# A two-layer diffusion backbone on one core: late small loads, turned rows modulated from PSUM, root norms behind attention

## The chip, the core and the metric

The kernel runs on one core of one Trainium2 chip, in one launch. The metric is the device time of that launch in microseconds (us). A core has five engines that work beside each other, each through its own queue in order: TensorE (PE; its weight loads are shown apart as PEld), VectorE (DVE), ScalarE (ACT), GpSimd (POOL) and SyncE (SP), which here issues nearly all DMAs. Matrix products land in PSUM; operands lie in SBUF. Differences under about 0.2% of the time are not counted as a change.

## The reference

512 latent tokens and 256 context tokens of width 1024 pass two layers. Each layer is a mixer and a squared-ReLU MLP, both between RMS norms, with a shift, a scale and a gate made from the conditioning vector. Layer 0 mixes by pooling, layer 1 by attention; after layer 1 only the latent tokens are needed.

```python
def rms_norm(x, g):
    xf = x.astype(jnp.float32)
    y = xf * lax.rsqrt(jnp.mean(xf * xf, axis=-1, keepdims=True) + EPS)
    return (y * g.astype(jnp.float32)).astype(x.dtype)
...
def modulate(h, shift, scale):
    return h * (1.0 + scale) + shift
...
    for i in range(DEPTH):
        last = i == DEPTH - 1
        j = i // N_MIXERS
        sh1, sc1, gt1, sh2, sc2, gt2 = ada_mods(c, w_ada[i], b_ada[i])
        csh1, csc1, cgt1, csh2, csc2, cgt2 = ada_mods(c_ctx, w_ada[i], b_ada[i])
        h_lat = modulate(rms_norm(x, g_mix_pre[i]), sh1, sc1)
        h_ctx = modulate(rms_norm(ctx, g_mix_pre[i]), csh1, csc1)
        if i % N_MIXERS == 0:
            y_lat = pool_mixer(h_lat, w_pool[j], pool_scale[j])
            y_ctx = None if last else pool_mixer(h_ctx, w_pool[j], pool_scale[j])
        else:
            y_lat, y_ctx = attention_mixer(h_lat, h_ctx, w_qkv[j], g_q[j], g_k[j], w_o[j], not last)
        x = x + gt1 * rms_norm(y_lat, g_mix_post[i])
        m_lat = sq_relu_mlp(modulate(rms_norm(x, g_mlp_pre[i]), sh2, sc2), w_mlp_in[i], w_mlp_out[i])
        x = x + gt2 * rms_norm(m_lat, g_mlp_post[i])
...
    return x
```

`ada_mods` is SiLU of the conditioning vector times `w_ada` (1024 x 6144 for each layer). `pool_mixer` is, for each of four groups of 256 channels, a windowed mean less the token itself (windows of 2, 4, 8 and 16 tokens), a 256 x 256 product and a scale by channel. Attention has 8 query heads and 2 key heads of 128, with RMS norms and rotary positions on queries and keys.

## The kernel before

Tokens lie in six tiles of 128 rows (`t` = 0 to 3 latent, 4 and 5 context), channels in eight blocks of 128 (`k`). Float32 operands of the large products are split in a high part (rounded) and a low part (the rest); a product is then three matmuls: high by high, high by low, low by high. In tile names `ra` and `rb` hold such halves, `acc` and `work` float32 results, `raw` freshly loaded weights, `units` split weights.

The program has these stages, in us of the profiled execution:

- *Front* (0 to about 102). The conditioning maps come as 1 MB loads of `w_ada`, called units (scale, shift and gate: SC1, SH1, GT1 for the mixer, SC2, SH2 for the MLP). `ada_mm` multiplies them into `psada`, `ada_turn` transposes that on VectorE, `ada_sel` and `ada_add` make columns `mods`, and `avec` (gain times one plus scale). Means by band matrices land in `psm`, the mixer's products in `pspool`. `pool_m` copies a row tile of `pspool` to `acc`, `pool_q` takes its root mean square on ScalarE, `pool_b` multiplies it by the gate and `pool_r` adds it to the stream. `turn_c` scales a row tile by its own norm, `turn_pair` transposes two row tiles on PE into `psx`, `turn_ev` copies that to `acc`, `modulated` applies scale and shift, `placed` splits it into `hH` and `hL` (the `ra<-acc` rows). The first inner product of the MLP follows in two chunks: chunk 0 is the first four row tiles (`psin`, 512 wide), chunk 1 the last two (256 wide).
- *First MLP* (102 to 600), a Strassen-like scheme whose products read `units`.
- *Queries, keys, values and attention* (600 to 776). `q_a` projects a chunk of queries into `psq`, `q_e` and `q_b` norm and rotate it; `q_head` transposes a head (`pq`), `s_scores` makes scores (`pss`) and their exponential, `s_norm` divides by the sum, `s_turn` transposes (`pspt`), `s_values` multiplies by the values (`po`).
- *Output projection, norm, and the first inner product of the second MLP* (776 to 838), *second MLP* (838 to 1135), *tail* (to 1164): the last row tile's norm, residual and output DMAs.

What stands where in the front and in attention's output is a table of planned times: `st.at(time, function, ...)` collects calls, and `Steps.run` issues them in the order of these times. `pin` and the flag `fixed` hold the resulting order on an engine; elsewhere a scheduler decides. DMAs go through SP's queue in order with eight semaphores in rotation. Raw weights of the front come from a ring of four tiles (`rawe`), two of SH2's loads from another of three (`rawp`).

The row norms after attention and at the end are the mean square (ScalarE) and a power of -0.5 on GpSimd:

```python
    def rstd(ss, parts):
        r = sm_tile("rs")
        gp.tensor_tensor(out=r[:, 0:1], in0=ss[:, parts + 3:parts + 4], in1=nhalf[:, 0:1], op=ALU.pow)
        return r
```

Of the kernel before, what the change touches and what calls it, by code (L numbers as in the profile page):

```python
# [17 lines left out]
P = 128  # L18
# [35 lines left out]
def backbone(ctx: ExitStack, tc, x, c, ctx_in, c_ctx, w_ada, b_ada, g_mix_pre, g_mix_post,  # L54
# [152 lines left out]
    def mean_square(src, ss, n):  # L207
        z = sc.activation(junk[:, 0:src.shape[-1]], src, AF.Square, scale=float(D) ** -0.5, accum_out=ss[:, n:n + 1])
        sc.activation(ss[:, n + 4:n + 5], ss[:, n:n + 1], AF.Identity, bias=ss[:, n + 3:n + 4] if n else eps)
        return z  # L210
# [8 lines left out]
    def row_root(key, src):  # L219
        roots[key] = ss = sm_tile("ss")  # L220
        sc.activation(junk, src, AF.Square, scale=float(D) ** -0.5, accum_out=ss[:, 0:1])
        sc.activation(ss[:, 1:2], ss[:, 0:1], AF.Sqrt, bias=eps)
# [36 lines left out]
    sy.dma_start(pr1[0:96, :], row(b_ada))  # L259
    sy.dma_start(pr1[96:112, :], row(g_mix_pre))  # L260
    sy.dma_start(pr1[112:128, :], row(g_mlp_pre))
# [3 lines left out]
    te.transpose(pp[:, 0:128], pr1, ident)  # L265
# [3 lines left out]
    ve.tensor_copy(cols, pp[:, 0:128])  # L269
# [8 lines left out]

    def ada_mm(i, m, c0, width, u):
        nk = 2048 // width  # L280
        raw = raw_load(w_ada[i, u * nk * P:(u + 1) * nk * P, m * D + c0:m * D + c0 + width]
                       .rearrange("(k p) n -> p k n", p=P), width,
                       rawp if (m, c0, u) in ((SH2, 0, 1), (SH2, 512, 0)) else None).rearrange("p (k n) -> p k n", n=width)
# [129 lines left out]

    def modulated_pair(t, i, s, hi, lo, works, wide, fine, on_act):
# [20 lines left out]
        for q in range(4):  # L435
# [13 lines left out]
            elif q % 2:  # L449
# [3 lines left out]
                ve.tensor_tensor(out=place(lo, ks), in0=split2(h), in1=place(hi, ks), op=ALU.subtract)  # L453

    def last_pair(t, i, s, hi, lo, on_act):
        works, sh = [accv[:, t + u, :] for u in range(2)], (SH1, SH2)[s] * KT
        pss = [psB.tile([P, 2, 256], F32, tag="b", name="psx") for _ in range(KT // 2)]
        for u in range(2):
            for k in range(KT):
                te.transpose(pss[k // 2][:, k % 2, u * P:(u + 1) * P], works[u][:, k * P:(k + 1) * P], ident)  # L460
        for k in range(KT):
            src, h = pss[k // 2][:, k % 2, :], works[k // 4][:, 256 * (k % 4):256 * (k % 4) + 256]
            sa, b = avec[i][s][:, k, 0:1], mods[i][:, sh + k, 0:1]
            z = slice(t * P, (t + 2) * P)
            if on_act[k]:
                sc.activation(h, src, AF.Identity, scale=sa, bias=b)
            else:
                ve.tensor_scalar(out=h, in0=src, scalar1=sa, scalar2=b, op0=ALU.mult, op1=ALU.add)
            sc.copy(hi[:, k, z], h)
            ve.tensor_tensor(out=lo[:, k, z], in0=h, in1=hi[:, k, z], op=ALU.subtract)  # L470
# [10 lines left out]
    def mean_mm(k, q, narrow=False):  # L481
# [8 lines left out]
        for i in range(n):  # L490
            v = 0 if i == 0 else (1 if i == n - 1 else 2)
            lo = max(i * P - HALO, 0)
            hi = min((i + 1) * P + HALO, n * P)
# [65 lines left out]
    def pool_mul(g):  # L559
        w4 = pw[0][:, 512 * g:512 * g + 512].rearrange("p (k n) -> p k n", n=256)  # L560
        ve.tensor_tensor(out=w4, in0=w4, in1=pw[1][:, 256 * g:256 * g + 256].unsqueeze(1).broadcast_to([P, 2, 256]),
                         op=ALU.mult)

    def pool_hi(g):
        z = slice(512 * g, 512 * g + 512)
        sc.copy(wpH[:, z], pw[0][:, z])
# [18 lines left out]
    def pool_q(t):  # L585
        row_root((0, t), accv[:, t, :])

    def pool_b(t, n0=0, n1=D):
        gated(t, accv[:, t, :], accv[:, t, n0:n1], n0, n1)
# [7 lines left out]
    def norm_r(t, half=False):  # L597
        y = yg.pop(t, accv[:, t, :])
        for h in range(2 if half else 1):
            residual(t, y, *((512 * h, 512 * h + 512) if half else (0, D)))  # L600

    def norm_s(t, half=False):
        if not half:
# [3 lines left out]
        for h in range(2):  # L607
            mean_square(xrow(t)[:, 512 * h:512 * h + 512], ss, h)
        rs[t] = rstd(ss, 2)

    def norm_c(t, act, pool, half=False):
        r = rs[t][:, 0:1]
# [17 lines left out]
    accp = acc.rearrange("p (q k n) -> p q k n", q=NT // 2, n=256)  # L630
# [3 lines left out]
    def turn_pair(q):  # L634
        src = accv[:, 2 * q:2 * q + 2, :]
        if q < 2:
            both = [psA.tile([P, 4, 256], F32, tag="a", name="psx") for _ in range(2)]
            pss = [both[kk // 2][:, 2 * (kk % 2):2 * (kk % 2) + 2, :] for kk in range(4)]
        else:
            pss = [psB.tile([P, 2, 256], F32, tag="b", name="psx") for _ in range(4)]  # L640
        for kk, ps in enumerate(pss):
            for k in range(2):
                for u in range(2):
                    pin(te.transpose(ps[:, k, u * P:(u + 1) * P], src[:, u, (2 * kk + k) * P:(2 * kk + k + 1) * P], ident),
                        q < 2)
        faced[q] = pss

    def turn_ev(q, on_act, kks=range(4)):
        for kk in kks:
            ps = faced[q][kk]  # L650
            pin((sc.copy if on_act[kk] else ve.tensor_copy)(accp[:, q, 2 * kk:2 * kk + 2, :], ps), q < 2)

    def modulated(k, ci, on):
        qs = (slice(0, 2), slice(2, 3))[ci]
        h = accp[:, qs, k, :]
        sa, b = avec[0][1][:, k, ci:ci + 1], mods[0][:, SH2 * KT + k, ci:ci + 1]
        if on is sc:
            z = sc.activation(h, h, AF.Identity, scale=sa, bias=b)
        else:
            z = on.tensor_scalar(out=h, in0=h, scalar1=sa, scalar2=b, op0=ALU.mult, op1=ALU.add)  # L660
        pin(z, ci == 0)

    def placed(k, ci, low):
        qs = (slice(0, 2), slice(2, 3))[ci]
        h = accp[:, qs, k, :]
# [23 lines left out]
    class Inner:  # L689
        def __init__(self, g, w, aH, aL, hid, chunks_of, ntok):  # L690
# [3 lines left out]
            self.ps, self.r = {}, {}  # L694

        def part(self, c, f, ks=range(KT), on=False):
# [5 lines left out]
            for k in ks:  # L702
                for n, (w, a) in enumerate(((wH, aH), (wH, aL), (wL, aH))):
# [944 lines left out]
```

## Time and profile before

| quantity | value |
|---|---|
| time, median of 3 runs (lowest to highest) | 1165.27 us (1164.26 to 1166.16) |
| the profiled execution, its own time | 1165.85 us |
| its span in the profile | 1164.0 us |
| DVE / ACT / POOL busy, share of the span | 80% / 56% / 7% |
| moved by DMA | 152.08 MB |
| granted TensorE clock | 1.00 in every stage |

The page of the profile gives busy time by engine, then the span in 40 slices, the chain of work that ended last, and the costliest groups. A row of a timeline is: start, duration, engine, line, operation, out<-in, partitions x elements and type, count, and in brackets how long the engine was idle just before and which tile of which engine released it. Nearly all lines read L68, a helper through which every instruction goes, so rows are told apart by their tiles. Here are the 40 slices of PE, DVE and DMA:

```profile
PE   6989999999999999999999999999999999999997
...
DVE  4787587889989899898768689977787779778875
...
DMA  9994132334434434444442300045344224314303
```

### The profile page before, as it was taken

Reading aid. Unit: us, or ns where it says so; the run is one execution under the profiler, and the core shown is the slowest. Engines: PE = TensorE matmul, PEld = TensorE weight load, DVE = VectorE, ACT = ScalarE, POOL = GpSimd, SP = SyncE. Lnnn points to the kernel's source line nnn. Section 1 sums busy time; section 2 is a strip of 40 time slices with the busy share of each in tenths; the row PEclk is TensorE's granted clock in tenths of the full one; section 3 lists DMA queues with packets and bytes.
Section 4 is the critical chain, followed back from the end, with each engine's and each line's share of the span. In section 5 each row is a group of like instructions: output and inputs, shape, how many; then the busy total and the mean of one; then the engine's idle time right before and its main releaser. Section 6 shows DMA issues by size and latency. Waiting matters only on the chain. (4 is left out here: it accounts for less than half of the span.)

```text
span 1164.0 us, 15687 instructions
## 1 busy us (share of the span) xinstructions
PE 1137.8 (98%) x6026; PEld 981.5 (84%) x6026; DVE 936.0 (80%) x1540; ACT 649.4 (56%) x1152; POOL 80.7 (7%) x93
## 2 busy tenths in 40 slices
PE   6989999999999999999999999999999999999997
PEld 4659899989889988988888889988888888888886
DVE  4787587889989899898768689977787779778875
ACT  5586655545335434555795468862775436435524
POOL 1052000000000000000232210102000000000000
PEclk9999999999999999999999999999999999999999
DMA  9994132334434434444442300045344224314303
GB/s 337 399 334 162 49 104 84 125 114 143 160 127 145 145 113 145 140 135 146 183 152 79 120 1 1 14 139 170 131 140 150 70 75 145 109 37 146 109 31 114
DMA packets 95161, 152.08 MB, mean 131 GB/s; under 512 B 2880, under 2 KB 67952, under 8 KB 95088
## 3 DMA queue, kind: packets, MB, share of 16 engines
q1 hardware_dynamic: 94992, 151.07, 37.7%
q8 instruction: 47, 0.77, 0.3%
q14 instruction: 26, 0.21, 0.1%
q10 hardware_dynamic: 96, 0.02, 0.0%
HBM read 141.65 MB, written 9.44 MB: 130 GB/s over the span
## 5 line engine op out<-in xcount | busy, mean ns | idle before, releaser
L68 PE MATMUL pso<-units,rb 128*128 128x512 f32 x1152 | 277.2, 392 | 0.0
L68 PEld LDWEIGHTS pso<-units,rb 128*128 128x128 f32 x1152 | 214.9, 188 | 41.6
L68 DVE TENSOR_TENSOR acc<-acc,pso 128x512 f32<-128x512 f32 x192 | 128.9, 684 | 61.5 <-PE pso L68 61.4
L68 DVE SCALAR_TENSOR_TENSOR rows<-raw,cond,rows 128x256 f32<-128x256 f32 x280 | 122.3, 486 | 0.7
L68 PE MATMUL psin<-ra 128*128 128x512 f32 (+1 forms) x424 | 112.2, 369 | 0.0
L68 PE MATMUL psin<-ra,rb 128*128 128x512 f32 (+1 forms) x384 | 103.5, 362 | 3.6 <-DVE ra L68 1.8
L68 ACT CAST units<-raw 128x1024 fp32r<-128x1024 f32 (+2 forms) x71 | 70.7, 1018 | 39.9 <-PE pso L68 21.7
L68 DVE TENSOR_TENSOR units<-raw,units 128x1024 fp32r<-128x1024 f32 (+2 forms) x69 | 82.7, 1208 | 12.5 <-ACT units L68 12.4
L68 PE MATMUL psin<-rb,ra 128*128 128x384 f32 (+1 forms) x324 | 90.6, 356 | 0.0
L68 PEld LDWEIGHTS psin<-ra 128*128 128x128 f32 x424 | 77.8, 188 | 11.3 <-DVE work L68 0.3
L68 ACT ACTIVATE work<-psin 128x512 f32<-128x512 f32 (+3 forms) x66 | 36.2, 550 | 85.9 <-PE psin L68 78.7
L68 PE MATMUL psin<-ra,units 128*128 128x384 f32 x432 | 82.7, 336 | 0.4 <-ACT psin L68 0.4
L68 PE MATMUL pso<-units,pairs 128*128 128x512 f32 x336 | 82.3, 389 | 0.0
L68 PEld LDWEIGHTS psin<-ra,rb 128*128 128x128 f32 x384 | 66.9, 189 | 17.1 <-DVE ra L68 3.3
L68 POOL TENSOR_TENSOR rs<-ss,nhalf 128x1 f32<-128x1 f32 x30 | 21.2, 708 | 855.1 <-ACT ss L68 852.2
L68 PEld LDWEIGHTS psin<-ra,units 128*128 128x128 f32 x432 | 76.3, 188 | 3.1 <-ACT psin L68 0.5
L68 PEld LDWEIGHTS pso<-units,pairs 128*128 128x128 f32 x336 | 63.1, 188 | 13.1
L68 PE MATMUL psin<-sums,units 128*128 128x384 f32 x336 | 63.8, 336 | 0.0
L68 PEld LDWEIGHTS psin<-rb,ra 128*128 128x128 f32 x324 | 58.6, 188 | 5.6
L68 ACT COPY acc<-pso 128x512 f32<-128x512 f32 x68 | 38.0, 589 | 41.5 <-PE pso L68 41.4
L68 PEld LDWEIGHTS psin<-sums,units 128*128 128x128 f32 x336 | 59.0, 188 | 1.4
L68 ACT CAST rb<-raw 128x2048 fp32r<-128x2048 f32 (+2 forms) x20 | 27.0, 1349 | 58.0 <-PE pso L68 55.7
(223 smaller groups left out, 2151.6 us busy)
## 6 DMA issues: line engine op xcount, KB each, us to landing
raw<-in_w_ada SPq DMA_DIRECT2D x48, 1024.0 KB, 5.4
raw<-in_w_mlp_in SPq DMA_DIRECT2D x32, 1024.0 KB, 5.3
raw<-in_w_mlp_out SPq DMA_DIRECT2D x32, 1024.0 KB, 5.9
raw<-in_w_qkv SPq DMA_DIRECT2D x6, 1024.0 KB, 5.1
spill<-xl SPq DMA_DIRECT2D x8, 512.0 KB, 5.6
xl<-spill SPq DMA_DIRECT2D x8, 512.0 KB, 7.5
raw<-in_w_o SPq DMA_DIRECT2D x4, 1024.0 KB, 4.9
xl<-in_x SPq DMA_DIRECT2D x4, 512.0 KB, 6.9
```

Source lines behind the costliest of these rows:

```text
L68: z = made(*args, **kw)
```

## The change

1. *Loads.* `b_ada`, `g_mix_pre` and `g_mlp_pre` are loaded behind the two units of SC1's first half, and transposed (`small_turn`) when they are needed. Both loads of SH2's first half use `rawp`.
2. *Mixer.* The band products take only as many columns as their window reaches (`halo = 1 << g` in place of a fixed one). `pool_mul` and two of the four `pool_hi` go to GpSimd. Row tiles 3, 4 and 5 of the mixer are not copied out of PSUM: the root mean square and the gating read `pspool`.
3. *Turned rows.* `turn_ev` is gone. `modulated` reads `psx` in PSUM, one 128 x 256 piece for each `k` and pair of row tiles, 12 on ScalarE and 12 on VectorE (before: 512 wide pieces on three engines for chunk 0, eight 256 wide pieces on GpSimd for chunk 1). `first_part` issues, for each `k`, the matmuls that don't read the low half ahead of those that do. The table of times is rewritten around it.
4. *Attention.* The last query chunk is copied from PSUM by `q_rest`; its squares stand behind four of the exponentials, and its norm and rotation go to GpSimd. Behind the last exponential stands one square root on a single column, which loads ScalarE's table for roots. One of the four tiles of probabilities (`pbuf`) moves to another part of `acc`.
5. *Norms behind attention.* The norms of the output stage and of the end are a square root on ScalarE and a reciprocal on VectorE. Two low halves of the earlier pair are held back behind the residual of the last row tile (`late`), nine matmuls of chunk 0 are kept back until the last transposes are out (`hold`), and modulates alternate between the engines.
6. *Tail.* The last row tile leaves in three DMAs (512, 256, 256 columns) in place of two.

```diff
+    def settle(t):
+        if t in pending:
+            rs[t] = sm_tile("rs")
+            ve.reciprocal(rs[t][:, 0:1], pending.pop(t))
...
-        sc.activation(ss[:, n + 4:n + 5], ss[:, n:n + 1], AF.Identity, bias=ss[:, n + 3:n + 4] if n else eps)
+        sc.activation(ss[:, n + 4:n + 5], ss[:, n:n + 1], AF.Sqrt if root else AF.Identity, bias=ss[:, n + 3:n + 4] if n else eps)
...
+                if (i, s, q) == (1, 1, 3):
+                    late.extend((place(lo, z), h[:, z.start - 4:z.stop - 4], place(hi, z)) for z in (slice(4, 6), slice(6, 8)))
...
-        ve.tensor_tensor(out=w4, in0=w4, in1=pw[1][:, 256 * g:256 * g + 256].unsqueeze(1).broadcast_to([P, 2, 256]),
+        gp.tensor_tensor(out=w4, in0=w4, in1=pw[1][:, 256 * g:256 * g + 256].unsqueeze(1).broadcast_to([P, 2, 256]),
...
     def pool_b(t, n0=0, n1=D):
-        gated(t, accv[:, t, :], accv[:, t, n0:n1], n0, n1)
+        if t not in mix:
+            gated(t, accv[:, t, :], accv[:, t, n0:n1], n0, n1)
+        else:
+            halves = lambda z: z.rearrange("p (q n) -> p q n", q=2)
+            ve.tensor_tensor(out=halves(accv[:, t, :]), in0=mix.pop(t), in1=halves(gate[:, slot[t], :]), op=ALU.mult)
...
-    def modulated(k, ci, on):
-        qs = (slice(0, 2), slice(2, 3))[ci]
-        h = accp[:, qs, k, :]
+    def modulated(q, k, on):
+        h, ps, ci = accp[:, k // 2, k % 2, q, :], faced[q, k // 2][:, k % 2, :], q // 2
         sa, b = avec[0][1][:, k, ci:ci + 1], mods[0][:, SH2 * KT + k, ci:ci + 1]
         if on is sc:
-            z = sc.activation(h, h, AF.Identity, scale=sa, bias=b)
+            sc.activation(h, ps, AF.Identity, scale=sa, bias=b)
...
+    def first_part(c, k):
+        first[0].final = 1
+        for terms in ((0, 2), (1,)):
+            for f in range(2):
+                first[0].part(c, f, (k,), False, terms)
...
-    ada_units(SH2, 512, 512, (72.9, 73.9), 76.5, 77.9, 78.6)
+    ada_units(SH2, 512, 512, (70, 73.9), 74.8, 75.75, 76)
...
+    def q_rest(ch, t):
+        d = q32[:, t, 512 * ch:512 * ch + 512]
+        ve.tensor_copy(d, pj[ch, t])
+        pj[ch, t] = d
...
-        head_norm(ps, r, 4, 0, t, q32[:, t, 512 * ch:512 * ch + 512])
+        head_norm(ps, r, 4, 0, t, q32[:, t, 512 * ch:512 * ch + 512], gp if exps and t == NL - 1 else ve)
...
+        at(33.6, lambda: sc.activation(sm_tile("sm")[:, 7:8], smx[len(steps) - 1][:, 1:2], AF.Sqrt))
...
-        for n0, n1 in ((0, 512), (512, D)):
+        for n0, n1 in ((0, 512), (512, D)) if t < NL - 1 else ((0, 512), (512, 768), (768, D)):
```

On VectorE, at the end of the front, where the scale and shift columns are made (`psada` transposed, then `mods` and `avec`) and the first turned rows are modulated, before and then now:

```order
L68 STREAM_TRANSPOSE work<-psada 128x512
L68 TENSOR_TENSOR acc<-acc,gate 128x1024
L68 STREAM_TRANSPOSE work<-psada 128x512
L68 RECIPROCAL rs<-ss 128x1
L68 SCALAR_TENSOR_TENSOR xr<-acc,rs,xr 128x1024
L68 TENSOR_TENSOR rb<-raw,rb 128x512 x2
L68 TENSOR_TENSOR mods_96<-psada,cols 128x16
L68 SCALAR_TENSOR_TENSOR avec_99<-mods_96,cols 128x16
L68 TENSOR_TENSOR mods_96<-psada,cols 128x8
L68 COPY acc<-psx 128x512
L68 TENSOR_SCALAR acc<-acc,avec_99,mods_96 128x2x256
L68 TENSOR_TENSOR ra<-acc,ra 128x2x2x128
```

```order
L68 STREAM_TRANSPOSE work<-psada 128x512
L68 TENSOR_TENSOR acc<-pspool,gate 128x1024
L68 RECIPROCAL rs<-ss 128x1
L68 STREAM_TRANSPOSE work<-psada 128x512
L68 TENSOR_TENSOR mods_96<-psada,cols 128x16
L68 SCALAR_TENSOR_TENSOR avec_99<-mods_96,cols 128x16
L68 TENSOR_TENSOR mods_96<-psada,cols 128x8
L68 TENSOR_TENSOR rb<-raw,rb 128x512
L68 TENSOR_SCALAR acc<-psx,avec_99,mods_96 128x256 x2
L68 TENSOR_TENSOR ra<-acc,ra 128x2x2x128
```

The last residual (`xr<-acc,rs,xr`) and a low half of the MLP's weights (`rb<-raw,rb`) have moved behind the columns, and the copy out of `psx` is gone.

On PE, the order of the last shift units (`psada<-raw,cond`), the turned rows (`psx`), the first inner product in its chunks of 512 and 256, and the first matmuls of the MLP proper (`psin<-ra,units`), before and then now:

```order
L68 MATMUL psx<-ident,acc 128x128 x16
L68 MATMUL psada<-raw,cond 32x512 x8
L68 MATMUL psin<-ra,rb 128x512 x12
L68 MATMUL psada<-work,sel 32x2x4 x4
L68 MATMUL psin<-ra,rb 128x512 x24
L68 MATMUL psx<-ident,acc 128x128 x16
L68 MATMUL psin<-ra,rb 128x512 x12
L68 MATMUL psin<-ra,rb 128x256 x43
L68 MATMUL psin<-ra,units 128x384 x4
L68 MATMUL psin<-ra,rb 128x256 x5
L68 MATMUL psin<-ra,units 128x384 x92
```

```order
L68 MATMUL psada<-raw,cond 32x512 x4
L68 MATMUL psin<-ra,rb 128x512 x12
L68 MATMUL psada<-raw,cond 32x512 x4
L68 MATMUL psx<-ident,acc 128x128 x8
L68 MATMUL psada<-work,sel 32x2x4 x4
L68 MATMUL psin<-ra,rb 128x512 x6
L68 MATMUL psx<-ident,acc 128x128 x8
L68 MATMUL psin<-ra,rb 128x512 x18
L68 MATMUL psx<-ident,acc 128x128 x16
L68 MATMUL psin<-ra,rb 128x512 x12
L68 MATMUL psin<-ra,rb 128x256 x48
L68 MATMUL psin<-ra,units 128x384 x96
```

Chunk 0 has begun ahead of the last unit, the second half of the first two pairs' transposes stands between its matmuls, and chunk 1 is one piece of 48.

On ACT, at the end of attention, from the last exponentials (`gate,sm<-pss,sm` and `acc,sm<-pss,sm`) to the casts that the last products with the values need, before and then now:

```order
L68 ACTIVATE gate,sm<-pss,sm 128x768
L68 CAST units<-pspt 128x3x128 x2
L68 ACTIVATE acc,sm<-pss,sm 128x768
L68 CAST ra<-po 128x256
L68 CAST units<-pspt 128x3x128 x4
```

```order
L68 ACTIVATE gate,sm<-pss,sm 128x768
L68 CAST units<-pspt 128x3x128 x2
L68 ACTIVATE acc,sm<-pss,sm 128x768
L68 ACT_TABLE_LOAD
L68 ACTIVATE sm<-sm 128x1
L68 CAST ra<-po 128x256
L68 CAST units<-pspt 128x3x128 x4
```

The table load and the one-column root stand between the last exponential and the casts.

270 lines of the change are left out of this document (153 added, 117 removed).

## The prediction

> **What bounds the kernel now.** I read the page first, then the busy time by stage, then each engine's timeline in the stages where TensorE is not full.
>
> ```profile
> PE 1137.8 (98%) x6026; PEld 981.5 (84%) x6026; DVE 936.0 (80%) x1540; ACT 649.4 (56%) x1152; POOL 80.7 (7%) x93
> ...
> 60.00:70.00 10.00, 10.00 (x88) 6.88 (x84) 8.04 (x14) 8.69 (x18) 5.70 (x2) 1.00 0.91 316
> 70.00:80.00 10.00, 7.33 (x81) 4.46 (x73) 9.36 (x16) 7.68 (x15) 3.85 (x4) 1.00 1.01 335
> 80.00:90.00 10.00, 8.85 (x41) 6.01 (x41) 7.98 (x17) 8.49 (x16) 5.73 (x3) 1.00 0.99 372
> 90.00:102.60 12.60, 11.87 (x84) 10.96 (x84) 9.44 (x17) 7.83 (x15) 6.47 (x8) 1.00 0.30 118
> 102.60:600.00 497.40, 497.00 (x2517) 445.41 (x2517) 419.54 (x736) 267.42 (x421) 16.02 (x14) 1.00 0.38 129
> 822.00:838.00 16.00, 14.75 (x117) 13.77 (x116) 11.81 (x22) 12.62 (x28) 1.88 (x3) 1.00 0.09 34
> ```
>
> After the stretch and its length the columns are the busy time of PE, PEld, DVE, ACT and POOL. PE is the bound over the whole (98%) and most plainly in the first MLP (497.00 of 497.40 us): nothing that the change does beside full PE work there is worth anything, and a microsecond by which that stage starts earlier is a microsecond of the end. What can be won lies where PE has gaps: the end of the front (70 to 102.6), the start and end of attention, the step into the second MLP (1.25 us idle in 822 to 838), and the tail.
>
> **The front.** The rows of VectorE and of PE there:
>
> ```profile
> 66.17 1.21 DVE L68 COPY acc<-pspool 128x1024 f32<-128x1024 f32 x1
> ...
> 71.38 0.76 DVE L68 TENSOR_SCALAR acc<-xl,rs 128x1024 f32<-128x1024 f32 x1
> ...
> 72.68 1.57 DVE L68 TENSOR_TENSOR acc<-acc,gate 128x1024 f32<-128x1024 f32 x1
> ...
> 74.81 0.12 DVE L68 RECIPROCAL rs<-ss 128x1 f32<-128x1 f32 x1
> ...
> 77.49 0.16 DVE L68 TENSOR_TENSOR mods<-psada,cols 128x16 f32<-128x16 f32 x1
> ...
> 77.85 0.68 DVE L68 COPY acc<-psx 128x512 f32<-128x512 f32 x1
> ...
> 81.33 0.71 DVE L68 STREAM_TRANSPOSE work<-psada 128x512 f32<-128x512 f32 x1
> ...
> 82.01 0.53 DVE L68 TENSOR_SCALAR acc<-acc,avec,mods 128x512 f32<-128x512 f32 x1
> ...
> 88.75 1.90 DVE L68 TENSOR_TENSOR ra<-acc,ra 128x512 fp32r<-128x512 f32 x3 [1.33 <-ACT ra L68]
> ```
>
> ```profile
> 74.93 0.25 PE L68 MATMUL psada<-work,sel 128*32 128x8 f32 x8 [1.78 <-DVE rs L68]
> ...
> 77.01 1.92 PE L68 MATMUL psada<-raw,cond 128*32 128x512 f32 x16
> ...
> 90.75 1.91 PE L68 MATMUL psx<-ident,acc 128*128 128x128 f32 x16
> ...
> 102.66 1.57 PE L68 MATMUL psin<-ra,units 128*128 128x384 f32 x8
> ```
>
> PE finished the last shift unit at 78.93 (77.01 + 1.92), but VectorE transposed it only at 81.33. VectorE was idle for 10.00 - 9.36 = 0.64 us in 70 to 80: it is late because its queue is full, not because data is missing. The last low half of chunk 0 ends at 88.75 + 1.90 = 90.65. So VectorE's chain sets chunk 0. It was idle for 1.96 us in 60 to 70 and for 2.02 in 80 to 90.
>
> *What goes.* From VectorE up to 90.65: the mixer copy (1.21), two evictions of turned rows (2 x 0.68), three modulates of 512 (about 3 x 0.53): 4.2 us. From ScalarE: two mixer copies, six evictions, three modulates. *What comes:* modulates straight from PSUM, with these durations from the same form elsewhere in this trace:
>
> ```profile
> L68 DVE TENSOR_SCALAR acc<-psx,avec,mods x21: 535/540/545, 590.6 to 830.8; 128x256 f32<-128x256 f32 x21
> L68 ACT ACTIVATE acc<-psx,mods,avec x19: 547/563/575, 589.2 to 831.4; 128x256 f32<-128x256 f32 x19
> ```
>
> Eight of the sixteen for chunk 0 stand on VectorE, 8 x 0.54 = 4.3, and the scaling of the last row comes to it from ScalarE (0.76 by the row at 71.38). So VectorE's work stays about level (+0.9, which its idle time just before holds); what changes is when it is done. The gating no longer stands behind a copy, the transposes of the scale and shift units stand ahead of the last residual, and the first modulates (from 77.85 on) depend on nothing but these. Laying the new queue out by these durations from 61.7 on, I get the scale and shift columns at 72.9 to 73.7 (now 77.49), and the last low half at 87.8 to 89.4, which is 1.3 to 2.9 earlier; take 2.1.
>
> Then chunk 1. Now its transposes stand on PE behind all of chunk 0 (90.75, 1.91 us), and GpSimd paces it:
>
> ```profile
> 92.47 6.47 POOL L68 TENSOR_SCALAR acc<-acc,avec,mods 128x256 f32<-128x256 f32 x8 [4.49 <-ACT acc L68]
> 98.39 3.14 PE L68 MATMUL psin<-ra,rb 128*128 128x256 f32 x24 [0.73 <-DVE ra L68]
> ```
>
> In the new order they stand ahead of the last twelve matmuls of chunk 0, where PE waits anyway, and two engines share the modulates. I count 1.91 + 0.73 = 2.6, less a part for a PE that then follows VectorE's low halves: 2.5. **Front: 4.6.** Bounds: if VectorE's queue is as late as now and only the 0.73 and a little of the transposes go, 1; if PE's whole idle time of 70 to 102.6 but the transpose chain goes (2.67 + 1.15 + 0.73 with the 1.91), 6. The first MLP behind it is one full PE queue, so it arrives whole. The small loads that now follow the first two scale units, and these units' earlier issue, I cost at nothing: the DMA engines stay full up to 90 (shares 1.01 and 0.99), with the same bytes. The scalings moved to GpSimd (four, about 1.46 each, price below) and its two casts lie beside waits for weights; without that cover they would cost at most a matmul group's delay, inside the lower bound.
>
> **Attention.**
>
> ```profile
> 687.88 1.31 PE L68 MATMUL pss<-rb 128*128 128x384 f32 x6 [0.94 <-ACT acc L68]
> 681.79 0.69 DVE L68 TENSOR_TENSOR work<-psq,rs 128x512 f32<-128x512 f32 x1
> ```
>
> At its start the norm and rotation of the last query chunk stand on VectorE between the first softmaxes (this row and four more, 2.8 us), and PE waits for an exponential. The change leaves one 0.69 copy there. The reductions come earlier, so the 0.94 should go and a little of the shorter waits around it: **1.1** (0 if PSUM banks, not VectorE, hold the exponentials; 2 if all five products came off PE's path but this copy). The norm goes to GpSimd, where it is needed by the fifth head's transposes:
>
> ```profile
> 703.68 0.93 ACT L68 ACTIVATE gate<-pss,sm 128x768 f32<-128x768 f32 x1
> 713.49 0.60 PE L68 MATMUL pq<-ident,acc 128*128 128x128 f32 x4
> L68 POOL TENSOR_TENSOR units<-raw,units 128x512 fp32r<-128x512 f32 x3 | 4.3, 1460 | 3.1 <-ACT units L68 3.1
> L68 POOL TENSOR_TENSOR rs<-ms,nhalf 128x4 f32<-128x4 f32 x8 | 9.0, 1126 | 0.7
> ```
>
> The last of its squares stands behind the exponential at 703.68, so about 705.2; then mean and power (1.1 by its row, and under half of that for the mean, an estimate), three products of 512 (3 x 1.46) and two of 256 (half each, an estimate from the same row): 705.2 + 1.5 + 5.9 = 712.6, against 713.49. It fits, by 0.9 us; both shift with the earlier start. I cost it at nothing.
>
> At the end a table load and one root stand ahead of the casts that PE waits for:
>
> ```profile
> 46.42 1.28 ACT L68 ACT_TABLE_LOAD   x1
> 47.72 0.29 ACT L68 ACTIVATE ss<-ss,phase 128x1 f32<-128x1 f32 x1
> ...
> 764.21 0.37 ACT L68 CAST ra<-po 128x256 fp32r<-128x256 f32 x1 [0.40 <-PE po L68]
> 766.09 2.42 PE L68 MATMUL po<-units,rb 128*128 128x256 f32 x18 [0.45 <-DVE units L68]
> ```
>
> 1.28 + 0.29 less the 0.40 of idle is 1.17, and PE already waits here; VectorE, slower than ScalarE on this tile, catches up a little: **cost 1.0** (0.7 to 1.2). The Trainium skill, "ScalarE: Activation LUTs", section "What ACT_TABLE_LOAD costs", gives 1283 ns for the load and about 1380 ns of drain beside it, 2.66 us in all; by it this term would be 2.4 and the predicted time 1159.5. The trace has the load at 1.28 and the next activation 0.02 us behind its end, so the load alone is taken.
>
> **Into the second MLP, and the tail.**
>
> ```profile
> 824.77 1.22 DVE L68 TENSOR_TENSOR rb<-acc,ra 128x1024 fp32r<-128x1024 f32 x1
> 828.46 0.49 DVE L68 TENSOR_SCALAR acc<-acc,rs 128x512 f32<-128x512 f32 x1 [1.81 <-POOL rs L68]
> 831.07 0.50 PE L68 MATMUL psin<-ra,rb 128*128 128x256 f32 x2 [0.97 <-ACT ra L68]
> 1158.48 0.29 ACT L68 ACTIVATE ss<-ss 128x1 f32<-128x1 f32 x1
> 1158.91 0.55 POOL L68 TENSOR_TENSOR rs<-ss,nhalf 128x1 f32<-128x1 f32 x1 [4.51 <-ACT ss L68]
> 1159.49 1.42 DVE L68 SCALAR_TENSOR_TENSOR xl<-work,rs,xl 128x512 f32<-128x512 f32 x2 [0.59 <-POOL rs L68]
> ```
>
> The low half at 824.77 stands between the two residual halves; moved behind them it frees 1.2 us of this chain, and the power on GpSimd with its two handovers becomes a root and a reciprocal (0.12 by the row at 74.81), another 0.5 to 0.8. So the last scaling is ready about 2 us before 828.46. Nine matmuls (9 x 0.12 = 1.1) that PE now does before the transposes are kept for the wait behind them, which covers the 0.97. What is late next is the low halves of chunk 1. PE's idle there is 1.25, with issue gaps 2.3: **2.0** (1 to 2.2). In the tail, 1158.77 (end of ScalarE) to 1159.49 becomes two short handovers and the reciprocal, some 0.2: **0.5** (0.2 to 0.7); a third, smaller output transfer leaves no later than the second does now.
>
> **Sum.** 4.6 + 1.1 - 1.0 + 2.0 + 0.5 = 7.2; ends 1.0 and 10.2. The profiled execution took 1165.85 (span 1164.0), so 1158.65 for its like; it lies 0.58 above the median of 1165.27, which gives 1158.1.
>
> **Rivals.**
> - *VectorE keeps the front.* Its work there is no smaller, and the gating from 72.68 took 1.57 beside GpSimd's casts. If the new queue ends as late as now, the front gives 1.0: 3.6 in all, **1161.7**. For it: 0.64 idle in 70 to 80. Against: 1.96 idle just before, and chunk 1's transposes move whatever VectorE does.
> - *It does not do what it says.* DMA sets the columns, chunk 1 is bound by low halves, and attention's start is held by banks: 1.0 + 0 - 1.0 + 1.5 + 0.3 = 1.8, **1163.5**. Against: the 2.4 us between 78.93 and 81.33, in which the data was there.
> - *Slower: GpSimd's norm holds PE.* PE is in order, and the fifth head's transposes have everything behind them. The rotation's products have pieces of 32 columns, a form that GpSimd shows nowhere here. The margin is 0.9; past it each microsecond of GpSimd is one of the end. To be 0.2% slower, it must be 0.9 + 7.2 + 2.3 = 10.4 late, 16 us in place of 5.9. At half of that, 8 us late, the time is **1165.2**; at 12 us late, 1169.2.
> - *The drain of that rule* comes with the load: 1159.5.
>
> **Chances.** Forecast 0.66 (own range 1155 to 1161; the drain's 0.04 lies in it too), VectorE keeps the front 0.15, does not do what it says 0.09, GpSimd holds PE to no gain or worse 0.06 (0.04 slower). About 0.2% (2.3 us) is what a measurement of this kernel can tell from no change. Faster is the forecast, the drain and the first rival, 0.85; same 0.11; slower 0.04. For 8 in 10 the range reaches from the sum's far side to the first rival: 1154.5 to 1162.5.
>
> **What would show it.** The scale columns (mods<-psada, 128x16) near 73.5, the last low half of chunk 0 by 89.4, the first matmul on units near 97.5. At attention, no wait of PE for ScalarE near 687, none before pq of the fifth head, one of about 1.4 at po after the table load. No wait over 0.3 between the last transposes and chunk 1 of the second MLP. It is wrong if the front's end moves by under 2 us, or if a group behind GpSimd shows a wait of PE.

## The result, and the profile after

| | before | changed kernel |
|---|---|---|
| median | 1164.84 us (4 runs, 1164.26 to 1166.16) | 1158.01 us (4 runs, 1157.76 to 1158.42) |
| profiled execution | 1165.85 us, span 1164.0 | 1157.76 us, span 1155.9 |
| ratio | | 0.994, 95% interval 0.9923 to 0.9957 |

The medians are 6.8 us apart; the sum forecast 7.2, and 1158.1 as the time. The two profiled executions are 8.1 us apart: that of the kernel before lay 1.0 above its median, that of the changed kernel 0.25 below. In what follows gains by stage are read from the two profiles, so they add up to 8.1, which is 1.3 more than the medians show.

Busy time by engine, and by stage, of the changed kernel (columns as before: stretch, length, PE, PEld, DVE, ACT, POOL, clock, DMA share):

```profile
PE 1134.6 (98%) x6026; PEld 980.2 (85%) x6026; DVE 938.3 (81%) x1551; ACT 644.4 (56%) x1150; POOL 74.3 (6%) x82
...
60.00:70.00 10.00, 10.00 (x102) 7.30 (x99) 9.50 (x17) 8.51 (x20) 6.81 (x4) 1.00 1.06 373
70.00:80.00 10.00, 9.95 (x75) 6.36 (x74) 9.61 (x21) 4.28 (x9) 4.85 (x4) 1.00 1.06 388
80.00:90.00 10.00, 10.00 (x60) 8.71 (x59) 9.71 (x22) 9.65 (x24) 0.00 (x0) 1.00 0.85 345
90.00:102.00 12.00, 12.00 (x85) 12.00 (x84) 8.57 (x12) 9.92 (x15) 0.00 (x0) 1.00 0.27 87
```

VectorE has as much to do as before in all (938.3 against 936.0), but in 60 to 70 it is busy for 9.50 us in place of 8.04, and in 80 to 90 for 9.71 in place of 7.98: the same work stands earlier. PE's gaps of 2.67 and 1.15 us in 70 to 90 are gone. A busy PE is not yet a quick one: what counts is when the first matmul of the MLP proper comes. VectorE's and PE's timelines at the rows that the prediction showed:

```profile
70.65 0.14 DVE L68 TENSOR_TENSOR mods<-psada,cols 128x16 f32<-128x16 f32 x1
...
77.35 0.72 DVE L68 STREAM_TRANSPOSE work<-psada 128x512 f32<-128x512 f32 x1 [0.24 <-PE psada L68]
...
84.83 1.29 DVE L68 TENSOR_TENSOR ra<-acc,ra 128x512 fp32r<-128x512 f32 x2 [0.25 <-ACT ra L68]
```

```profile
72.04 1.07 PE L68 MATMUL psada<-raw,cond 128*32 128x512 f32 x8
73.15 3.14 PE L68 MATMUL psin<-ra,rb 128*128 128x512 f32 x12
76.22 1.06 PE L68 MATMUL psada<-raw,cond 128*32 128x512 f32 x8
...
84.94 1.91 PE L68 MATMUL psx<-ident,acc 128*128 128x128 f32 x16
86.60 8.75 PE L68 MATMUL psin<-ra,rb 128*128 128x512 f32 x60
95.19 7.10 PE L68 MATMUL psin<-ra,units 128*128 128x384 f32 x40
```

The columns are made at 70.65 (before 77.49), the last shift unit is transposed as soon as PE has it (0.24 of wait, before 2.4 us late), chunk 0's last low half ends at 86.12 (before 90.65). The fifth matmul on units, which stood at 102.66, stands at 95.89.

The same matmul in both profiles gives what each stage brought:

| landmark on PE | before | after | gain so far | of this stage | forecast |
|---|---|---|---|---|---|
| fifth matmul on units (front) | 102.66 | 95.89 | 6.77 | 6.8 | 4.6 |
| last projection of queries | 678.34 | 671.58 | 6.76 | 0.0 | 0 |
| last matmul of the scores | 761.04 | 753.53 | 7.51 | 0.75 | 1.1 |
| first matmul of the output projection | 776.16 | 769.59 | 6.57 | -0.93 | -1.0 |
| first 512-wide matmul of the second MLP | 837.98 | 830.07 | 7.91 | 1.3 | 2.0 |
| last matmul of the output | 1157.65 | 1149.86 | 7.79 | -0.1 | 0 |
| end of the span | 1164.00 | 1155.90 | 8.10 | 0.3 | 0.5 |

The first MLP passes the front's gain on to the hundredth, as a full PE queue should. At attention's start PE's wait of 0.94 is gone, and two shorter ones stand there:

```profile
676.86 1.33 PE L68 MATMUL pss<-rb 128*128 128x384 f32 x6 [0.44 <-ACT gate L68]
...
683.84 1.31 PE L68 MATMUL pss<-rb 128*128 128x384 f32 x6 [0.32 <-ACT xr L68]
```

The end of attention, on ScalarE and PE, and GpSimd's norm with the PE row that reads what it made:

```profile
756.32 1.28 ACT L68 ACT_TABLE_LOAD   x1
757.62 0.20 ACT L68 ACTIVATE sm<-sm 128x1 f32<-128x1 f32 x1
...
762.03 0.37 ACT L68 CAST ra<-po 128x256 fp32r<-128x256 f32 x1 [2.38 <-PE po L68]
```

```profile
758.59 0.55 PE L68 MATMUL pspt<-ident,xr 128*128 128x128 f32 x3 [0.94 <-DVE ra L68]
759.58 2.41 PE L68 MATMUL po<-units,rb 128*128 128x256 f32 x18 [0.45 <-DVE units L68]
```

```profile
703.00 1.31 POOL L68 TENSOR_TENSOR acc<-work 128x512 f32<-128x512 f32 x1
...
705.96 0.60 PE L68 MATMUL pq<-ident,acc 128*128 128x128 f32 x4
```

The wait of 0.45 at `po` was there before; new is the 0.94 ahead of it, behind a cast that now waits for the table. GpSimd is done at 704.31, 1.65 us ahead of PE.

In the tail the reciprocal follows the root at once, and the residual leaves in three pieces:

```profile
1151.03 0.15 DVE L68 RECIPROCAL rs<-ss 128x1 f32<-128x1 f32 x1
1151.22 1.54 DVE L68 SCALAR_TENSOR_TENSOR xl<-work,rs,xl 128x512 f32<-128x512 f32 x3
```

The residual starts 1.36 us after the start of the last matmul (before: 1159.49 - 1157.65 = 1.84), but only 0.3 of these 0.5 us reach the end.

### The profile page after: what moved, and what is told of

Its sections match the earlier page's. It is cut to its first block, busy times and chain, and to the rows that moved or that the text cites. A ratio compares the mean times of both kernels' runs of the same rounds, so it can differ in the third digit from the quotient of the medians.

```text
span 1155.9 us, 15680 instructions
## 1 busy us (share of the span) xinstructions
PE 1134.6 (98%) x6026; PEld 980.2 (85%) x6026; DVE 938.3 (81%) x1551; ACT 644.4 (56%) x1150; POOL 74.3 (6%) x82
## 4 chain that ended last, share of the span: by engine, by line
PE 94%; ACT 2%; DVE 2%; DMA 1%; issue 0%; SPq 0%; POOL 0%; DVEq 0%; ACTq 0%
PE pso L68 36%; PE psin L68 35%; PE psq L68 7%; PE psy L68 4%; PE po L68 3%; PE pss L68 2%; PE psada L68 1%; PE pspt L68 1%; PE pspool L68 1%; PE psx L68 1%; PE psg L68 1%; DVE ra L68 1%; ACT junk L68 1%; ACT ra L68 1%; DMA raw<-in_w_ada 1%
## 5 line engine op out<-in xcount | busy, mean ns | idle before, releaser
L68 ACT ACTIVATE work<-work 128x768 f32<-128x768 f32 (+1 forms) x50 | 41.4, 831 | 28.8 <-DVE work L68 28.3
```

The lines of the kernel that those rows point to most:

```text
L68: z = made(*args, **kw)
```

## The experiments

The total came out as forecast with terms that were not: the front brought 2.2 us more, the others together 1.3 less. The first question is what made the front so good, the second whether the small terms are what they seem. Except where a median is given, each run was executed once and is read by the fifth matmul on units (95.89 in the changed kernel) and the later landmarks. Profiles of kernels that don't differ in the front put that matmul between 95.89 and 96.35, so front differences under 0.5 us are not read.

In runs 2, 3 and 6 the granted TensorE clock was not 1.00 throughout the front. It fell to 0.50 for 3.41 us. In the order of the runs (columns as above, GB/s last):

```profile
75.41:78.82 3.41, 3.41 (x11) 2.23 (x8) 2.07 (x4) 0.58 (x2) 1.40 (x1) 0.50 1.09 357
...
75.18:78.59 3.41, 3.41 (x20) 1.63 (x22) 2.75 (x8) 2.70 (x5) 0.00 (x0) 0.50 1.06 401
...
73.13:76.54 3.41, 3.41 (x24) 2.93 (x22) 3.34 (x8) 1.04 (x3) 3.41 (x2) 0.50 1.08 366
```

Shortly before, PE had waited 2.29, 1.78 and 2.46 us. The kernel before has the same wait of 1.78 us (at 74.93) and kept its full clock, so no run settles whether the wait brings the half clock. A price read from these runs holds both, and the two are told apart below.

**1. Where the small loads stand.** The changed kernel with

```diff
+    sy.dma_start(pr1[0:96, :], row(b_ada))
+    sy.dma_start(pr1[96:112, :], row(g_mix_pre))
+    sy.dma_start(pr1[112:128, :], row(g_mlp_pre))
...
-    st.at(13.9, small_loads)
```

> The changed kernel with the three small loads put back ahead of the first scale units. Theory A (the weight units set the front's end: they land 1.7 us earlier at 54 and 3.1 us earlier at 77 than before the change): all units land 1 to 2 us later than in the changed kernel, and the fifth matmul on units, at 95.9 in the changed kernel, comes 1 to 2 us later. Theory B (only the engines' queues set it, the landings have slack): the units land later and that matmul stays within 0.3 us of 95.9.

The matmul came at 96.11, the time was 1158.11 us. The run doesn't tell the theories apart, because the units didn't land later: the first half of SC1 landed at 18.05 in place of 17.78, the later units within 0.2 us of the changed kernel. What it shows is that the place of the small loads is worth nothing that can be seen.

**2. The ring of SH2's first load.** The changed kernel with

```diff
-                                       rawp if (m, c0) == (SH2, 0) else None).rearrange("p (k n) -> p k n", n=width)
+                                       rawp if (m, c0, u) in ((SH2, 0, 1), (SH2, 512, 0)) else None).rearrange("p (k n) -> p k n", n=width)
```

> The changed kernel with the first load of the MLP's first shift half taken from the ring of four again, where it waits for PE to free a tile. Theory A: it and all behind it land 1 to 1.5 us later, and the fifth matmul on units comes 1 to 1.4 us later than 95.9. Theory B: within 0.3 us.

The matmul came at 99.88, 4.0 us later, the end with it (1161.93 us). SP now waits for PE to free a tile, once for 6.2 us, and issues this load at 59.78 in place of 53.17; the weights of the MLP and the last shift half stand behind it in SP's queue. PE's timeline in that run:

```profile
71.37 1.09 PE L68 MATMUL psx<-ident,acc 128*128 128x128 f32 x8
74.75 1.34 PE L68 MATMUL psada<-raw,cond 128*32 128x512 f32 x8 [2.29 <-DMA raw<-in_w_ada]
76.02 4.30 PE L68 MATMUL psin<-ra,rb 128*128 128x512 f32 x12
80.25 1.07 PE L68 MATMUL psada<-raw,cond 128*32 128x512 f32 x8
```

PE's order is fixed, with the last units ahead of and among chunk 0, so a late landing is a wait of the whole queue. With the 2.29 us of that wait PE stands 2.7 us behind the changed kernel (74.75 in place of 72.04). The other 1.3 us come from the 20 matmuls behind it, at the clock of 0.50: the twelve of chunk 0 took 4.30 us in place of 3.14. Theory A holds, with a price beyond its own range, 2.7 us without the half clock and 4.0 with it. The condition is that of the kernel before, so the first load of SH2's second half uses `rawp` in this run, too.

**3. The kernel before with the new loads.** Its three small loads and `ada_load` as in the changed kernel; it also has the changed kernel's ring for SH2, which the expectation does not say. Against the kernel before:

```diff
-    sy.dma_start(pr1[0:96, :], row(b_ada))
-    sy.dma_start(pr1[96:112, :], row(g_mix_pre))
-    sy.dma_start(pr1[112:128, :], row(g_mlp_pre))
...
+    st.at(13.9, ada_load, 0, SC1, 0, 512, 0)
+    st.at(13.9, ada_load, 0, SC1, 0, 512, 1)
+    st.at(13.9, small_loads)
+    st.at(13.9, pool_weights)
...
-    st.at(19.3, pool_weights)
+    st.at(20.55, small_turn)
```

> The kernel before with the order of the first loads alone changed (small loads behind the first two scale units, mixer weights behind these). Theory A: the fifth matmul on units, at 102.7 before, comes 1.5 to 2 us earlier. Theory B: less than 0.5 us earlier, since VectorE's queue sets that kernel's front whatever the loads do.

The last shift unit landed at 74.97 (77.71 before), and the matmul came at 101.58, 1.1 us earlier than in the profile of before, between the two theories; the time was 1164.86 us, beside 1165.01 for the kernel before and 1164.84 for its median, so the times show no gain. VectorE's and PE's timelines there:

```profile
42.26 0.17 DVE L68 TENSOR_TENSOR mods<-psada,cols 128x16 f32<-128x16 f32 x1 [0.49 <-PE psada L68]
...
76.27 0.17 DVE L68 TENSOR_TENSOR mods<-psada,cols 128x16 f32<-128x16 f32 x1
...
80.24 0.71 DVE L68 STREAM_TRANSPOSE work<-psada 128x512 f32<-128x512 f32 x1
```

```profile
76.55 2.91 PE L68 MATMUL psada<-raw,cond 128*32 128x512 f32 x16
```

The same columns in the kernel before:

```profile
43.50 0.17 DVE L68 TENSOR_TENSOR mods<-psada,cols 128x16 f32<-128x16 f32 x1 [0.48 <-PE psada L68]
```

The last loads come 2.7 us earlier and VectorE's rows there 1.1. But VectorE is 1.24 us ahead already at 42.26, about as much as the context rows landed earlier (1.16, run 4), so what the later loads gain adds nothing here. Nor does the half clock hide a gain: the last units' matmuls took 2.91 us in place of 1.92 and ended at 79.46, and VectorE's queue came to their transpose at 80.24 without a wait. With the old queue the loads alone bring little, while with the new queue one of them issued late costs 2.7 (run 2): the earlier loads pay only with the new queue.

**4. A second profile of the kernel before.** No edit.

> The kernel before, unchanged, for a second profile. In its first profile every load from the second on lands 1.2 to 1.5 us later than in any other kernel's profile, the context rows too, which stand ahead of everything that changed. Theory C (that lateness belongs to the one execution): here the context rows land near 10.9 and the fifth matmul on units comes near 101.5, not 102.7, so that the change's gain in the front is 5.5 us, not 6.8. Rival (it belongs to the order of loads): 102.7 again.

In this execution (1171.29 us) the granted clock fell to 0.83 in 20 to 40 us and to 0.87 in 80 to 90, so nothing behind 20 us is used. Ahead of that the clock was 1.00, and the context rows landed at 11.96, as in the first profile (12.02) and not as in the others (10.4 to 11.1). The lateness belongs to this kernel and not to one execution, so theory C falls; but run 1, whose small loads stand as in this kernel, and run 3, which is this kernel but for its loads, don't show it. What causes it stays open.

**5. Turned rows of chunk 1 late.** The changed kernel with

```diff
-                      (82.3, 2, range(4))):
+                      (85.75, 2, range(4))):
...
-        z = 83.5 + .8 * (k // 4) * 2 + .4 * (k % 2)
+        z = 86.95 + .8 * (k // 4) * 2 + .4 * (k % 2)
...
-        st.at(87.5 + .72 * k, first_part, 1, k)
+        st.at(90.95 + .72 * k, first_part, 1, k)
```

> The changed kernel with the last pair's transposes behind all of chunk 0 again, as before, and what follows them moved with it. If chunk 1's share of the front is what the prediction made of it (2.5 us), the fifth matmul on units comes 2 to 2.6 us later than 95.9. If PE, which shows no idle time in 72 to 102 in the changed kernel, does the same work in another order, under 0.7.

The matmul came at 98.10, 2.2 us later, the time was 1160.02 us: chunk 1's term (2.5) was sized right. PE shows why, with no work left to do behind the transposes while they are modulated:

```profile
88.23 1.91 PE L68 MATMUL psx<-ident,acc 128*128 128x128 f32 x16
91.27 4.62 PE L68 MATMUL psin<-ra,rb 128*128 128x256 f32 x34 [1.13 <-ACT ra L68]
```

**6. The mixer's last rows through a copy.** The changed kernel with

```diff
-    for t, on, z, q in ((1, sc, 41.2, 42.25), (2, sc, 42.2, 45.5), (0, ve, 47.4, 49), (3, None, 0, 54.45),
-                        (4, None, 0, 61.31), (5, None, 0, 64.25)):
+    for t, on, z, q in ((1, sc, 41.2, 42.25), (2, sc, 42.2, 45.5), (0, ve, 47.4, 49), (3, sc, 54.4, 54.45),
+                        (4, ve, 61.2, 61.31), (5, sc, 64.2, 64.25)):
```

> The changed kernel with the mixer's row tiles 3, 4 and 5 copied out of PSUM again (ScalarE, VectorE, ScalarE) ahead of root and gating. If VectorE's queue still sets the columns, 1.0 to 1.3 us later at the fifth matmul on units. If the landing of the shift units sets it, which the run with the ring of four spoke for, under 0.4.

The matmul came at 100.29, 4.4 us later, the time was 1162.5 us: more than either theory. The loads were on time (last shift unit at 74.90). Its timelines of ScalarE, VectorE and PE:

```profile
66.52 1.06 ACT L68 ACTIVATE junk<-acc 128x1024 bf16<-128x1024 f32 x1 [1.87 <-DVE acc L68]
```

```profile
65.27 1.21 DVE L68 COPY acc<-pspool 128x1024 f32<-128x1024 f32 x1
...
71.88 0.70 DVE L68 STREAM_TRANSPOSE work<-psada 128x512 f32<-128x512 f32 x1
```

```profile
72.63 0.34 PE L68 MATMUL psada<-work,mods 128*32 128x8 f32 x16 [2.46 <-DVE work L68]
72.90 1.79 PE L68 MATMUL psx<-ident,acc 128*128 128x128 f32 x8
...
74.85 1.90 PE L68 MATMUL psx<-ident,acc 128*128 128x128 f32 x8
```

VectorE's copy waits its turn, ScalarE's root waits for the copy (1.87), VectorE's reciprocal and gating wait for the root, and the transpose of the scale units stands behind them: at 71.88 in place of 68.24, 3.6 us late for 1.2 us of VectorE's time and two copies of 1.0 on ScalarE. The chain runs through two queues in turn, and this is what a sum of one engine's durations misses. PE is 3.1 us behind the changed kernel when its wait ends (72.63 in place of 69.54). The other 1.3 of the 4.4 us come behind that, at the clock of 0.50, where two groups of transposes took 1.79 and 1.90 us in place of 1.09. Without the half clock the price is about 3.1, still more than either theory.

**7. The last query chunk's norm on VectorE again.** `q_rest` left out, `q_e` and `q_b` as before and at their old times:

```diff
-        pj[ch, t] = ps, head_rstd(ps, 4, [exps[i] for i in (4, 6, 8, 10)] if exps else None)
+        pj[ch, t] = ps, head_rstd(ps, 4)
...
-        head_norm(ps, r, 4, 0, t, q32[:, t, 512 * ch:512 * ch + 512], gp if exps and t == NL - 1 else ve)
+        head_norm(ps, r, 4, 0, t, q32[:, t, 512 * ch:512 * ch + 512])
...
-                if c == 2 * NL - 1:
-                    st.at(107.6, q_rest, ch, t)
-                st.at([71.2, 76.4, 81.6, 86.8, 92, 97.2, 102.4, 132][c], q_e, ch, t)
-                st.at([71.5, 76.7, 81.9, 87.1, 92.3, 97.5, 102.7, 132.1][c], q_b, ch, t)
+                st.at([71.2, 76.4, 81.6, 86.8, 92, 97.2, 102.4, 107.6][c], q_e, ch, t)
+                st.at([71.5, 76.7, 81.9, 87.1, 92.3, 97.5, 102.7, 107.9][c], q_b, ch, t)
```

> The changed kernel with the norm of the last query chunk on VectorE among the first softmaxes again, as before. If it is worth what the trace shows between the last projection matmul and the late scores (0.75 us), the matmul that ends attention comes 0.7 to 0.8 us later than in the changed kernel. If the exponentials there are held by PSUM banks, under 0.2.

From the last projection (0.4 us later than in the changed kernel) to the end of attention it lost 1.7 us, as PE waits twice for an exponential:

```profile
682.85 1.31 PE L68 MATMUL pss<-rb 128*128 128x384 f32 x6 [1.31 <-ACT xr L68]
...
693.10 1.33 PE L68 MATMUL pss<-rb,units 128*128 128x384 f32 x6 [0.91 <-ACT xr L68]
```

That is more than the 0.75 by which the change beats the kernel before, whose queues had another order around the same norm. The mechanism holds, and the rival with the PSUM banks, under 0.2, does not.

**8. GpSimd's norm made longer.** The changed kernel with

```diff
-        for o in range(2):
+        for o in (0, 1) * (1 if on is ve else 4):
```

> The changed kernel with the two rotation products of GpSimd's query norm issued four times instead of once (same result), six more instructions of 0.9 to 1.05 us: GpSimd would end at 710 instead of 704.3, where PE stands at the fifth head's transposes at 705.96. If the slower rival's mechanism holds, PE waits there for 3.9 to 4.6 us and the end of attention comes as much later. If the softmax work queued behind in PE can be made up, under 2 us.

The six extra instructions took 4.2 us in all, so GpSimd ended at 708.63. PE's wait for it was 0.25, and the end of attention came 1.0 us later against the last projection: the second branch. The scheduler had set other matmuls ahead of the last of the four transposes, the only one that waits for GpSimd, and PE did those first. Another wait of 0.29, for VectorE, stands at 709.30; which rows make up the rest of the 1.0 is not shown. GpSimd and PE:

```profile
699.93 7.33 POOL L68 TENSOR_TENSOR work<-work,acc 128x256 f32<-128x256 f32 x9
707.35 1.28 POOL L68 TENSOR_TENSOR acc<-work 128x512 f32<-128x512 f32 x1
```

```profile
708.69 0.33 PE L68 MATMUL pq<-ident,acc 128*128 128x128 f32 x1 [0.25 <-POOL acc L68]
```

**9. The power on GpSimd kept.** No roots behind attention, no table load; the held low halves and matmuls stay:

```diff
-            whole = c0 + width == D
+            whole = False
...
-            pending[t] = ss1[t][:, len(ps1[t]) + 4:len(ps1[t]) + 5]
+            rs[t] = rstd(ss1[t], 1 + len(ps1[t]))
...
-        at(33.6, lambda: sc.activation(sm_tile("sm")[:, 7:8], smx[len(steps) - 1][:, 1:2], AF.Sqrt))
...
```

> The changed kernel with the norms behind attention and at the end as a power on GpSimd again, without the table load; the held low halves and matmuls stay. By the prediction's terms: attention's end 0.9 us earlier, the step into the second MLP 0.5 to 0.8 later, the tail 0.5 later (0.3 by the trace): in all within 0.4 us of the changed kernel. If the power's handovers weigh more there than I made of them, over 0.5 us later in all.

Attention's end gained 0.95, the step into the second MLP lost 0.24, the tail 0.32: 0.4 us in favour of the power, where the table load stands now. In the step the root is worth under half of what was expected.

**10. Held work put back.** Low halves ahead of the residual, the nine matmuls in their place:

```diff
-                if (i, s, q) == (1, 1, 3):
-                    late.extend((place(lo, z), h[:, z.start - 4:z.stop - 4], place(hi, z)) for z in (slice(4, 6), slice(6, 8)))
-                else:
+                if True:
...
-                    for z in range(2):
-                        at(42.95, lambda z: pin(ve.tensor_tensor(out=late[z][0], in0=late[z][1], in1=late[z][2], op=ALU.subtract)), z)
-                    at(47.4, last_pair, 2, 1, 1, h1H, h1L, lambda: first1[0].part(0, 1, range(5, KT), True))
+                    at(47.4, last_pair, 2, 1, 1, h1H, h1L, lambda: None)
...
-            at((42.96, 42.97)[f], lambda *a: first1[0].part(*a), 0, f, range(KT - 3 * f))
+            at((42.96, 42.97)[f], lambda *a: first1[0].part(*a), 0, f)
```

> The changed kernel with the two low halves back ahead of the residual and the nine kept matmuls back in their place; roots stay. If they carry the step into the second MLP, PE waits for about 1 us behind the last transposes again and the first 512-wide matmul of that MLP comes 0.8 to 1.3 us later. If the root and the reciprocal carry it, under 0.4.

The first 512-wide matmul came 1.1 us later, with the old wait back on PE. The run puts back both at once, so it doesn't tell their shares apart.

```profile
824.40 0.51 PE L68 MATMUL psin<-ra,rb 128*128 128x256 f32 x2 [0.88 <-ACT ra L68]
```

**11 and 12. The table load in an idle gap.** It is issued by `root_set`, ordered behind the casts of the last step but two, where ScalarE waits 2.38 us for PE:

```diff
-            sc.copy(hi, ps)
+            turned[i] = sc.copy(hi, ps)
...
+    def root_set():
+        z = sc.activation(sm_tile("sm")[:, 7:8], smx[len(steps) - 1][:, 1:2], AF.Sqrt)
+        tc.add_manual_dep(z.ins, turned[len(steps) - 3].ins.name, ISSUE, reason="row order")
...
-        at(33.6, lambda: sc.activation(sm_tile("sm")[:, 7:8], smx[len(steps) - 1][:, 1:2], AF.Sqrt))
+        at(34.15, root_set)
```

> The changed kernel with the table load and the one-column root moved behind the next four casts of attention's end, into 2.4 us in which ScalarE is idle. If the load costs what it keeps from the casts (0.9 us between the last scores and the output projection), that stretch shortens by 0.8 to 1.0 us and nothing else moves. If a drain of about 1.4 us comes with the load, the later casts are late by some 0.5 us and the gain is 0.4 to 0.5. If PE's wait there has another cause (VectorE's divisions), under 0.2.

> The kernel with the table load behind the casts, timed. By its trace it is 0.9 us faster than the changed kernel, so 7.7 us under the kernel before, a ratio of 0.9934; under 0.2% against the changed kernel, which the times alone can't tell.

The output projection began at 768.65 in both profiles, 0.93 us earlier than in the changed kernel. ScalarE's timeline:

```profile
757.08 1.63 ACT L68 CAST units<-pspt 128x384 fp32r<-128x384 f32 x4
758.72 1.28 ACT L68 ACT_TABLE_LOAD   x1
760.02 0.20 ACT L68 ACTIVATE sm<-sm 128x1 f32<-128x1 f32 x1
761.09 0.37 ACT L68 CAST ra<-po 128x256 fp32r<-128x256 f32 x1 [0.87 <-PE po L68]
```

0.87 us of idle time are left behind it. Timed: 1156.91 us (5 runs, 1156.28 to 1157.21) beside 1165.38 (9 runs) of the kernel before, a ratio of 0.9924 (0.9911 to 0.9938). It is the best version seen, though the times alone can't tell it from the changed kernel (interval 0.9923 to 0.9957).

## Why the prediction came out

*What bounds the kernel.* Right. Only PE's gaps could be won, and what the front won went unchanged through the first MLP and the projections behind it (6.77 at the first units, 6.76 at the last projection).

*Front.* The mechanism was right, "VectorE's work stays about level; what changes is when it is done", and so was the mark: the columns' lateness was the queue's. The size was off: 6.8 in place of 4.6, above the bound of 6. The mis-sized term is chunk 0's, 2.1, measured 4.5 (its last low half at 86.12, before 90.65); chunk 1's 2.5 stands at 2.2 by run 5 and 2.3 by the rest of the profile (6.8 - 4.5).

About 1 of the 4.5 us lies ahead of the stretch that the prediction laid out from 61.7 on: VectorE's residual there ends at 60.77, before at 61.73. That is the size of the first loads' lateness in the kernel before (runs 3 and 4), which is unexplained, and by which the profile of that kernel also lies above its median. That it belongs to the change is not shown. Without it the front brought 5.8, within the bound of 6, and chunk 0's term 3.5, still more than the 2.1.

Two things were missing in that term. The chain of copy, root, reciprocal and gating through ScalarE and VectorE was counted as durations, while run 6 shows that its waits make a row of VectorE 3.6 us late. And the loads were costed "at nothing", with the same bytes in full engines as the reason. The bytes are the same, but SP's wait for PE held the order of their issue, and run 2 puts 2.7 us on one load alone, whose change of ring the prediction does not name. The small loads themselves were rightly costed at nothing (run 1). Runs 2, 5 and 6 take away 2.7, 2.2 and 3.1 without the half clock, together more than the whole 6.8: these parts hold the same end up, so their prices can't be added, and no part has a share of its own.

*Attention's start.* 1.1, measured 0.75. The mechanism is shown by run 7. The wait of 0.94 went, but PE still waits 0.44 for one exponential and now 0.32 for a later one.

*GpSimd's norm.* Costed at nothing with 0.9 us to spare; it had 1.65. The slower rival's price, one for one past the margin, did not hold for the kernel of run 8: it paid 1.0 us for 2.6 us past it (4.2 - 1.65), as its order gives PE other work.

*Attention's end.* Cost 1.0, measured 0.93, and run 11 shows it to be the load's place: in a wait of ScalarE it cost nothing. The Trainium skill ("ScalarE: Activation LUTs", section "What ACT_TABLE_LOAD costs") gives about 1380 ns of drain beside 1283 ns of load. The trace agrees with the load, 1.28 us in every place, and shows nothing of the drain: the next activation starts 0.02 us behind the load (757.62).

*Step into the second MLP.* 2.0, measured 1.3. That is about PE's idle time of 1.25 in that stretch; the 2.3 "with issue gaps", on which the 2.0 leans, is shown by no row. By run 10 the held low halves and matmuls carry 1.1, and by run 9 the root 0.24, not "another 0.5 to 0.8". The root is worth no more where the held work is missing: from the first matmul of the output projection to the first 512-wide one, run 10 (root, no held work) took 61.57 us and the kernel before (neither, and its modulates in the old order) 61.82. So the price of the power's handovers was too high by half or more; which of them it overstates stays open.

*Tail.* 0.5, measured 0.3: the residual starts 0.5 earlier, but its third piece takes 0.12 more (1.54 against 1.42), and the third DMA, behind two issues, is issued 0.14 us after the residual's end (before 0.03).

That the forecast met the median to 0.1 us is in part luck. The terms missed by +2.2 and -1.3, 0.9 together. Against that stand the 0.58 that the forecast took off because the profile of before lay above its median, and the 0.25 by which the profile of the changed kernel lay below its own.

## What to carry to other kernels

Where two engines hand a value back and forth, count the waits of the chain, not the durations of one queue: three copies of 1.0 to 1.2 us, put back into such a chain, made a row of VectorE 3.6 us late. Look for loads whose issue waits on a buffer that the busy engine frees, since everything behind them in that queue is late as well; and try parts together, because a part that does nothing alone may be what the others need. Read the granted clock of the very stretch before a wait is given a price: here 1.3 of 4.0 and 1.3 of 4.4 us were matmuls at half the clock. A fixed cost such as a table load belongs in a gap that the profile already shows, 2.4 us here, and not at the point where it is first possible.

## What the runs showed of the hardware

- A table load of ScalarE takes 1.28 us, with the next activation 0.02 us behind its end, at both places tried.
- GpSimd's two products of 128x512 float32 in the query norm took 1.04 and 1.29 us and its sum 1.31, against 1.46 for a difference of that size elsewhere. Its products of 256 columns in pieces of 32 took 1.10 us for the first and about 0.7 for the others (4.2 us for six).
- The granted clock fell to 0.50 in single stretches of 3.41 us in the front of runs 2, 3 and 6, each a little behind a wait of PE of 1.8 to 2.5 us; matmuls of 128x512 took 4.30 us for twelve there in place of 3.14. What starts this is not shown.
- The first loads of the kernel before move more slowly than the same loads of the other kernels (context rows at 12.0 in both its profiles, 10.4 to 11.1 in the others).
